# One mixture-of-experts stage: low halves on VectorE, all gates through DRAM, one ring of row tiles

## The chip, the cores and the metric

The kernel runs on one core of a Trainium2 chip. The metric is the device time of one execution in microseconds (us). A core has TensorE (PE, with its weight loads PEld), VectorE (DVE), ScalarE (ACT), GpSimd (POOL) and SyncE (SP); SP issues nearly all plain DMAs, POOL issues the indirect ones (gathers of table rows by index).

## The reference, cut to what matters

The model is two blocks of 512 tokens by 1024 features in float32. The change touches only the last layer of the second block, the retrieval of single-neuron experts, and what lies behind it:

```
q  = (t @ wq) ; sc = q . subkeys            # 512 tokens, 8 heads, 2 halves, 128 keys
s1,i1 = top_k(sc[half 0], 16) ; s2,i2 = top_k(sc[half 1], 16)
best,pos = top_k(s1 + s2, 16)               # of 256 sums
idx = e1 * 128 + e2 ; gate = softmax(best)  # 128 experts for each token, of 16384
act = gelu(u_tab[idx] . t) * gate
out = sum over the 128 of act * v_tab[idx]
```

## The kernel before

Every float32 product is made of three matmuls: an operand is split into a rounded high half (made by ACT, `hi`) and a low half, raw minus high (made by `lo`), and `mm3` adds high times high, high times low and low times high. `weight` (L266) loads one raw 128 x 1024 tile on SP's queue, makes the high half `wh` on ACT, and the low half `wl` on POOL, or on VectorE where the caller says so. L248 and L256 are the helper lines of the high and of the low half, whoever calls them.

The expert stage is `peer`. It treats the first 128 tokens and the other 384 (three groups `j` of 128) differently.

- Tokens 128 to 511 go the dense way: all 16384 experts in 128 blocks `b` of 128. `hidden(b)` multiplies the weight block `p_ut[b]` with the 384 tokens (24 matmuls of 384 columns into PSUM tile `H`) and ACT makes the gelu `Hg`. A dense gate matrix says how much each token wants of each expert. `gates` builds it, four tokens at a time (a gate group below): VectorE compares index rows with `iota` (tiles `o`, L1621, L1622, L1626), ACT scales two of the four (L1628), PE multiplies the one-hot tiles (`G`, L1629), ACT copies the result into `Gs` (L1630). There are 96 groups: three `j`, two halves of 64 tokens, 16 groups each; the halves use the two buffers `Gs0` and `Gs1`.
- Tokens 0 to 127 go the sparse way: `fetches` gathers, with indirect DMAs on POOL (L1566), 128 rows of `p_u` and 128 of `p_v`, each 128 x 1024; VectorE takes a dot product (L1571) or adds a scaled row to `y` (L1582).

Three parts follow each other. **Part A**, `topk`, to 2561 us: query products, maxima on VectorE. **Part B**, to about 2977 us: `decode` (indices and softmax), `gates`, and `hidden` of the first 72 blocks, each `Hg` written to DRAM (`dAct`). The gates of the first two `j` are written to DRAM (`dGate`), in eight writes of 512 KB for each half; those of the last `j` stay in `Gs0` and `Gs1`. **Part C**, to the end: for each block `b` one load of `p_v[b]`, the activation of the block (read back from `dAct` for b under 72, computed by `hidden` after that), times the gates, split (`ach`, `acl`), and 18 matmuls of 512 columns into six accumulators `acc`. The gate multiply is three VectorE instructions: 256 columns from `Gt` (L1479, read back for two blocks at a time) and twice 64 columns from `Gs0` and `Gs1` (L1482). In part C two of three `p_v` blocks have their low half on POOL, the third on VectorE; `p_ut` blocks always on POOL. About 1.15 rows are gathered per block at first, 3.03 per block from block 72, none after block 118.

The raw weights and the gathered rows share one ring of 7 tiles, `wr`; `wh` and `wl` have 4 tiles each. The program is written in the order of its stages; a scheduler then sets one fixed order for each engine and each queue, and every queue runs in order.

```
def lo(self, dst, src, hi, eng='dve'):
    e = self.nc.vector if eng == 'dve' else self.nc.gpsimd
    e.tensor_tensor(dst, src, hi.bitcast(F32), op=OP.subtract)
```

## Time and profile before

| | us |
|---|---|
| median of 3 runs (lowest, highest) | 3870.37 (3865.46, 3876.9) |
| the profiled execution: its time, its span | 3871.17, 3869.4 |
| busy in the span: PE, VectorE | 3500.6, 2833.6 |
| busy in the span: POOL, ACT | 1845.0, 1517.7 |
| mean granted TensorE clock | 0.953 of full |

What lies around the span is 1.8 us. The granted clock of a stretch is the mean over two levels: 1.0 is 2.4 GHz, 0.5 is 1.2 GHz. Busy times of PE are modelled and pipelined matmuls overlap, so its idle time is more telling than its busy time. A group's line names the line of the code, the engine, the operation, what it writes from what it reads with shapes, the count, the busy time in us, the mean of one in ns, and the idle time of the engine before it with what ended it. "DMA share" is the mean busy share of the core's 16 DMA engines.

### The profile page before, as it was taken

What the parts mean: (1) busy time and instruction counts of PE and PEld (TensorE: products, weight loads), DVE (VectorE), ACT (ScalarE), POOL (GpSimd) and SP (SyncE); (2) the same over time, 40 slices, a digit from 0 to 9 for tenths busy, and PEclk for the clock granted to TensorE, in tenths of its full rate; (3) what the DMA queues carried; (4) which work ended last, traced back from release to release, by engine and by line L of the source; (5) the groups of instructions that cost most, each with busy time, mean ns of one, the idle gap of its engine ahead of it and who ended that gap; (6) DMA issues with size and microseconds to landing.
All of it is one profiled execution on the core that took longest, in us unless ns stands there. A gap on an engine that the chain in (4) does not pass through costs nothing.

```text
span 3869.4 us, 51339 instructions
## 1 busy us (share of the span) xinstructions
PE 3500.6 (90%) x18415; PEld 2933.1 (76%) x18415; DVE 2833.6 (73%) x5128; ACT 1517.7 (39%) x2484; POOL 1845.0 (48%) x1039
## 2 busy tenths in 40 slices
PE   6889898999999669999999998997899999989988
PEld 4657667778888557788887976897798777777777
DVE  7895769777788893322496354889997899888884
ACT  4433573323323444323444443333676333222223
POOL 3763102222222444344346432566545676888773
PEclk9899898999999779999999998998999999999999
DMA  5442023344334444233323323245566898888782
GB/s 216 142 141 71 25 68 101 116 131 139 116 113 148 152 154 132 82 97 94 115 77 95 123 93 118 86 149 170 203 246 219 309 309 305 284 278 288 282 285 90
DMA packets 266992, 615.38 MB, mean 159 GB/s; under 512 B 39920, under 2 KB 132720, under 8 KB 263920
## 3 DMA queue, kind: packets, MB, share of 16 engines
q1 hardware_dynamic: 225232, 477.33, 37.1%
q0 software_dynamic: 36864, 134.23, 10.0%
q8 instruction: 145, 2.38, 0.3%
q10 hardware_dynamic: 4640, 0.53, 0.1%
q14 instruction: 111, 0.91, 0.1%
HBM read 539.26 MB, written 72.71 MB: 158 GB/s over the span
## 4 chain that ended last, share of the span: by engine, by line
PE 21%; DVE 9%; POOL 8%; issue 7%; DMA 4%; ACT 1%; POOLq 0%; ACTq 0%; DVEq 0%; SPq 0%
POOL wl L256 5%; PE mm L280 3%; PE mm L282 3%; PE mm L281 3%; POOL wr L1566 3%; DMA wr<-in_p_v_dram,idx 2%; PE H L282 2%; PE H L281 2%; PE H L280 2%; DVE o L1626 1%; PE acc L282 1%; PE acc L281 1%; PE acc L280 1%; PE G L1629 1%; DVE wr L1571 1%
## 5 line engine op out<-in xcount | busy, mean ns | idle before, releaser
L256 POOL TENSOR_TENSOR wl<-wr,wh 128x1024 fp32r<-128x1024 f32 x469 | 1172.4, 2503 | 1242.0 <-ACT wh L248 1137.0
L248 ACT ACTIVATE wh<-wr 128x1024 fp32r<-128x1024 f32 x512 | 536.8, 1053 | 724.5 <-PE mm L281 372.9
L280 PE MATMUL mm<-hh,wh 128*128 128x512 f32 (+1 forms) x1024 | 365.6, 362 | 25.1 <-DVE x L534 11.6
L282 PE MATMUL H<-wh,wl 128*128 128x384 f32 x1024 | 354.2, 346 | 17.8 <-POOL wl L256 16.8
L281 PE MATMUL mm<-hl,wh 128*128 128x512 f32 (+1 forms) x1024 | 366.3, 358 | 2.2 <-DVE hl L344 2.2
L282 PE MATMUL mm<-hh,wl 128*128 128x512 f32 (+1 forms) x1024 | 365.3, 358 | 1.6 <-POOL wl L256 1.6
L280 PE MATMUL H<-wh,wh 128*128 128x384 f32 x1024 | 349.9, 342 | 1.9 <-ACT Hg L1434 1.9
L281 PE MATMUL H<-wl,wh 128*128 128x384 f32 x1024 | 350.6, 342 | 0.0
L282 PE MATMUL acc<-wh,acl 128*128 128x512 f32 x768 | 310.1, 407 | 24.9 <-DVE acl L256 24.6
L280 PE MATMUL acc<-wh,ach 128*128 128x512 f32 x768 | 311.2, 405 | 20.7 <-ACT ach L248 20.7
L281 PE MATMUL acc<-wl,ach 128*128 128x512 f32 x768 | 308.3, 401 | 0.0
L1582 DVE SCALAR_TENSOR_TENSOR y<-wr,wgt,y 128x1024 f32<-128x1024 f32 x127 | 233.2, 1836 | 61.7 <-DMA wr<-in_p_v_dram,idx 61.3
L280 PE MATMUL mm<-fh,wh 128*128 128x512 f32 (+1 forms) x768 | 273.4, 357 | 5.0 <-DVE x L500 3.8
L281 PE MATMUL mm<-fl,wh 128*128 128x512 f32 (+1 forms) x768 | 273.5, 357 | 1.1 <-DVE fl L256 1.1
L282 PE MATMUL mm<-fh,wl 128*128 128x512 f32 (+1 forms) x768 | 272.3, 356 | 0.0
L280 PEld LDWEIGHTS mm<-hh,wh 128*128 128x128 f32 x1024 | 196.6, 193 | 64.6 <-DVE x L534 16.1
L1571 DVE SCALAR_TENSOR_TENSOR wr<-wr,tt 128x1024 f32<-128x1024 f32 x128 | 202.3, 1585 | 39.5 <-DMA wr<-in_p_u_dram,idx 25.2
L281 PEld LDWEIGHTS mm<-hl,wh 128*128 128x128 f32 x1024 | 197.3, 193 | 34.4 <-DVE hl L344 3.9
L282 PEld LDWEIGHTS mm<-hh,wl 128*128 128x128 f32 x1024 | 196.5, 192 | 30.7 <-POOL wl L256 2.4
L282 PEld LDWEIGHTS H<-wh,wl 128*128 128x128 f32 x1024 | 196.0, 191 | 27.6 <-POOL wl L256 27.4
L1566 POOL DMA_INDIRECT wr<-in_p_u_dram,idx x128 | 163.2, 1275 | 107.2 <-DVE wr L1571 42.1
L1566 POOL DMA_INDIRECT wr<-in_p_v_dram,idx x128 | 169.6, 1325 | 91.6 <-DVE y L1582 49.0
(684 smaller groups left out, 8519.4 us busy)
## 6 DMA issues: line engine op xcount, KB each, us to landing
wr<-in_mlp_w_dram SPq DMA_DIRECT2D x128, 512.0 KB, 3.6
wr<-in_p_ut_dram SPq DMA_DIRECT2D x128, 512.0 KB, 4.5
wr<-in_p_v_dram SPq DMA_DIRECT2D x128, 512.0 KB, 5.0
aw<-in_ada_w_dram SPq DMA_DIRECT2D x48, 512.0 KB, 3.6
wr<-in_ada_w_dram SPq DMA_DIRECT2D x32, 512.0 KB, 4.4
dGate<-Gs SPq DMA_DIRECT2D x32, 512.0 KB, 6.3
Gt<-dGate SPq DMA_DIRECT2D x64, 256.0 KB, 5.6
dAct<-Hg SPq DMA_DIRECT2D x72, 192.0 KB, 2.5
```

What stands on the lines that cost most here:

```text
L248: self.nc.scalar.activation(dst, src, AF.Copy, **({} if scale is None else {'scale': scale}))
L256: e.tensor_tensor(dst, src, hi.bitcast(F32), op=OP.subtract)
L280: mm(out, ah, bh, start=first, stop=False)
L281: mm(out, ah, bl, start=False, stop=False)
L282: mm(out, al, bh, start=False, stop=last)
L1566: gp.indirect_dma_start(out=r, out_offset=None, in_=tab, in_offset=bass.IndirectOffsetOnAxis(ap=idx[:, s:s + 1], axis=0))
L1571: v.scalar_tensor_tensor(r, r, 1.0, tt, op0=OP.mult, op1=OP.mult, accum_out=dots[:, s:s + 1])
L1582: v.scalar_tensor_tensor(y0, r, wgt[:, s:s + 1], y0, op0=OP.mult, op1=OP.add)
L1626: v.tensor_scalar(o1[:, t], iota, row, gate, op0=OP.is_equal, op1=OP.mult)
L1629: nc.tensor.matmul(p[:, t * 128:(t + 1) * 128], o2[:, t], o1[:, t], start=True, stop=True)
```

## The change

Five edits, in their effect on the program:

1. After `topk`, every low half of a weight is made on VectorE: 72 of `hidden` in part B, and in part C the 56 of `hidden` and the 85 of 128 `p_v` blocks that were on POOL. POOL keeps those of `topk` and the earlier layers.
2. The 16 multiplies of `decode` on 128 x 1024 tiles go from POOL to VectorE.
3. The gates of all three `j` go through DRAM: 16 more writes of 512 KB in part B.
4. In part C the gates of four blocks are read at once (768 KB per four blocks, before 256 KB per two), and the gate multiply of a block is one instruction of 384 columns, before three.
5. `Gs0` and `Gs1` end with part B. In their room part C has a ring of 13 tiles, `rw`, for raw `p_v` and `p_ut` blocks and gathered rows.

```diff
+        self.lo_eng = 'pool'
+        self.rows = None
...
-    def weight(self, ap, lo_eng='pool'):
-        raw = self.t(self.wp, [128, 1024], 'wr', F32, self.wb[0])
+    def row_tile(self):
+        pool, tag, bufs = self.rows or (self.wp, 'wr', self.wb[0])
+        return self.t(pool, [128, 1024], tag, F32, bufs)
+
+    def weight(self, ap, lo_eng=None):
+        lo_eng = lo_eng or self.lo_eng
+        raw = self.row_tile()
...
-            dG = tc.dram_tile([ND - 1, 2, 128, 128, 64], F32, name='dGate')
+            dG = tc.dram_tile([ND, 2, 128, 128, 64], F32, name='dGate')
...
-            G2 = [self.t(gp_, [128, 128, 64], f'Gs{i}') for i in range(2)]
             with ExitStack() as e1:
+                G2p = e1.enter_context(self.pool('pgs'))
+                G2 = [self.t(G2p, [128, 128, 64], f'Gs{i}') for i in range(2)]
...
                     cands = self.topk(tp, e2.enter_context(self.pool('pq', side='right')), hs)
+                self.lo_eng = 'dve'
...
-                        if j < ND - 1:
-                            for a in range(0, 128, 16):
-                                nc.sync.dma_start(dG[j, i, :, a:a + 16], G2[i][:, a:a + 16])
+                        for a in range(0, 128, 16):
+                            nc.sync.dma_start(dG[j, i, :, a:a + 16], G2[i][:, a:a + 16])
...
+                self.rows = e1.enter_context(self.pool('rows')), 'rw', 13
...
-                    if b % 2 == 0:
-                        G = self.t(tp, [128, 2 * (ND - 1), 2, 64], 'Gt', bufs=2)
-                        nc.sync.dma_start(G, dG[:, :, :, b:b + 2].rearrange('j i e a t -> e (j i) a t'))
+                    if b % 4 == 0:
+                        G = self.t(tp, [128, 2 * ND, 4, 64], 'Gt', bufs=2)
+                        nc.sync.dma_start(G, dG[:, :, :, b:b + 4].rearrange('j i e a t -> e (j i) a t'))
                         Gt.append(G)
-                    M = 128 * (ND - 1)
-                    Hm = H[:, :M].rearrange('e (j t) -> e j t', t=64)
-                    v.tensor_tensor(Hm, Hm, Gt[-1][:, :, b % 2], op=OP.mult)
-                    for i in range(2):
-                        ts = slice(M + 64 * i, M + 64 * i + 64)
-                        v.tensor_tensor(H[:, ts], H[:, ts], G2[i][:, b], op=OP.mult)
+                    Hm = H.rearrange('e (j t) -> e j t', t=64)
+                    v.tensor_tensor(Hm, Hm, Gt[-1][:, :, b % 4], op=OP.mult)
...
-                    wv = self.weight(I['p_v'][b * 128:(b + 1) * 128], 'pool' if b % 3 else 'dve')
+                    wv = self.weight(I['p_v'][b * 128:(b + 1) * 128])
...
-            r = self.t(self.wp, [128, D], 'wr', bufs=self.wb[0])
+            r = self.row_tile()
...
-                gp.tensor_tensor(oh.rearrange('p (h k) a -> p h k a', h=4), oh.rearrange('p (h k) a -> p h k a', h=4), atf[:, hs, i, None, :].to_broadcast([128, 4, K, K]), op=OP.mult)
+                v.tensor_tensor(oh.rearrange('p (h k) a -> p h k a', h=4), oh.rearrange('p (h k) a -> p h k a', h=4), atf[:, hs, i, None, :].to_broadcast([128, 4, K, K]), op=OP.mult)
```

The scheduler sets a new order from all this. In the rows below a name before `<-` is what is written, the names behind it what is read; numbers in names tell buffers apart.

TensorE at the end of part B, before (`H` is a block of `hidden`, `acc` the first block of part C):

```order
L281 MATMUL H_26456<-wl_20969,wh_26452 128x384
L282 MATMUL H_26456<-wh_20968,wl_26453 128x384
L280 MATMUL H_26456<-wh_20975,wh_26452 128x384
L281 MATMUL H_26456<-wl_20976,wh_26452 128x384
L282 MATMUL H_26456<-wh_20975,wl_26453 128x384
L280 MATMUL acc_26530<-wh_26553,ach_26547 128x512
L281 MATMUL acc_26530<-wl_26554,ach_26547 128x512
L282 MATMUL acc_26530<-wh_26553,acl_26548 128x512
L280 MATMUL acc_26531<-wh_26553,ach_26547 128x512
L280 MATMUL H_26490<-wh_20926,wh_26486 128x384
L281 MATMUL H_26490<-wl_20927,wh_26486 128x384
```

Before, all gate groups have gone by here, and the last block of `hidden` begins between the first matmuls of part C. The same place after, where the last block of `hidden` ends (`G` is one gate group):

```order
L289 MATMUL H_26509<-wh_20968,wl_26506 128x384
L287 MATMUL H_26509<-wh_20975,wh_26505 128x384
L288 MATMUL H_26509<-wl_20976,wh_26505 128x384
L289 MATMUL H_26509<-wh_20975,wl_26506 128x384
L1634 MATMUL G_23651<-o_4721_23652,o_4722_23653 128x128 x4
L1634 MATMUL G_23665<-o_4724_23666,o_4725_23667 128x128 x4
L1634 MATMUL G_23679<-o_4727_23680,o_4728_23681 128x128 x4
L1634 MATMUL G_23693<-o_4730_23694,o_4731_23695 128x128 x4
L1634 MATMUL G_23707<-o_4733_23708,o_4734_23709 128x128 x4
L1634 MATMUL G_23721<-o_4736_23722,o_4737_23723 128x128 x4
```

From there on the row holds 23 gate groups and no other matmul, to the first of part C:

```order
L1634 MATMUL G_23939<-o_4781_23940,o_4782_23941 128x128 x4
L1634 MATMUL G_23953<-o_4784_23954,o_4785_23955 128x128 x4
L1634 MATMUL G_23967<-o_4787_23968,o_4788_23969 128x128 x4
L287 MATMUL acc_26553<-wh_26574,ach_26568 128x512
L287 MATMUL acc_26554<-wh_26574,ach_26568 128x512
```

So `hidden` has moved ahead of the gates, and the last 23 groups stand alone.

SP's queue at the start of part C, before, with the semaphores that a DMA waits for (`DMAHW` with a digit is one of the eight that tell of landed SP transfers; `nf` is the weight of the final norm, `xf` the residual of the first 128 tokens):

```order
L270 DMA wr_26674<-in_p_v_dram 128x1024 [waits DMAHW6_49,Pool_49]
L1458 DMA dAct<-Hg_26334 128x384 [waits DMAHW7_49,Activation_49]
L270 DMA wr_26717<-in_p_v_dram 128x1024 [waits DMAHW0_49,Pool_49]
L1488 DMA nf_26536<-in_nf_w_dram 128x1024 [waits DMAHW1_49,PE_49]
L1490 DMA xf_26538<-dXs 128x8x128 [waits DVE_49,DMAHW2_49,PE_49,Activation_49]
L1530 DMA Hr_26540<-dAct 128x384 [waits DMAHW3_49,PE_49]
L1475 DMA Gt_26542<-dGate 128x4x128 [waits DMAHW4_49,PE_49]
L1530 DMA Hr_26557<-dAct 128x384 [waits DMAHW5_49]
```

The gate writes of the last `j` are not there, and five loads of `p_v` stand ahead of these rows. The same place after:

```order
L1463 DMA dGate<-Gs_4137_21001 128x1024 [waits DMAHW7_49]
L1463 DMA dGate<-Gs_4137_21001 128x1024 [waits DMAHW0_49]
L1493 DMA nf_26559<-in_nf_w_dram 128x1024 [waits DMAHW4_49,DMAHW5_49,DMAHW3_49,DMAHW6_49,DMAHW2_49,DMAHW7_49,DMAHW1_49,DMAHW0_49]
L1495 DMA xf_26561<-dXs 128x8x128 [waits PE_49]
L1535 DMA Hr_26563<-dAct 128x384
L1484 DMA Gt_26565<-dGate 128x6x256 [waits DVE_49,PE_49]
L277 DMA rw_26572<-in_p_v_dram 128x1024
L1535 DMA Hr_26578<-dAct 128x384
```

The last sixteen transfers ahead of `nf` are the gate writes of the last `j`, and `nf` now waits for all eight semaphores; the reads of `dAct`, of the gates and of `p_v` stand behind it.

VectorE in part C beyond block 72, before (L1571 is a dot product with a gathered row, L1479 and L1482 the gate multiply):

```order
L1571 SCALAR_TENSOR_TENSOR wr_30852,dots_20995<-wr_30852,tt_20892 128x1024
L1479 TENSOR_TENSOR Hg_30702<-Hg_30702,Gt_30635 128x256
L1482 TENSOR_TENSOR Hg_30702<-Hg_30702,Gs_4136_20997 128x64
L1482 TENSOR_TENSOR Hg_30702<-Hg_30702,Gs_4137_20998 128x64
L1571 SCALAR_TENSOR_TENSOR wr_30855,dots_20995<-wr_30855,tt_20892 128x1024
L256 TENSOR_TENSOR acl_30714<-Hg_30702,ach_30713 128x384
L1571 SCALAR_TENSOR_TENSOR wr_30883,dots_20995<-wr_30883,tt_20892 128x1024
L256 TENSOR_TENSOR wl_30889<-wr_30886,wh_30888 128x1024
L1571 SCALAR_TENSOR_TENSOR wr_30925,dots_20995<-wr_30925,tt_20892 128x1024
L1479 TENSOR_TENSOR Hg_30775<-Hg_30775,Gt_30783 128x256
```

The same stretch after, where L1576 and L1487 are those lines:

```order
L1487 TENSOR_TENSOR Hg_30497<-Hg_30497,Gt_30287 128x384
L1576 SCALAR_TENSOR_TENSOR rw_30814,dots_20995<-rw_30814,tt_20892 128x1024
L258 TENSOR_TENSOR acl_30507<-Hg_30497,ach_30506 128x384
L258 TENSOR_TENSOR wl_30613<-rw_30610,wh_30612 128x1024
L1576 SCALAR_TENSOR_TENSOR rw_30856,dots_20995<-rw_30856,tt_20892 128x1024
L1576 SCALAR_TENSOR_TENSOR rw_30859,dots_20995<-rw_30859,tt_20892 128x1024
L258 TENSOR_TENSOR wl_30678<-rw_30675,wh_30677 128x1024
L1487 TENSOR_TENSOR Hg_30568<-Hg_30568,Gt_30576 128x384
L1576 SCALAR_TENSOR_TENSOR rw_30887,dots_20995<-rw_30887,tt_20892 128x1024
L258 TENSOR_TENSOR acl_30580<-Hg_30568,ach_30579 128x384
L258 TENSOR_TENSOR wl_30684<-rw_30681,wh_30683 128x1024
```

The gate multiply is one row, and two low halves `wl` of 1024 columns stand in the queue for each block, between the rows that take gathered tiles.

## Rows read from the trace of the kernel before

**Rows 1.** The window view, six stretches: engines' busy time and instructions, granted clock, DMA share, GB/s

```profile
2561.00:2640.00 79.00, 61.24 (x334) 60.31 (x333) 67.89 (x88) 25.79 (x34) 56.66 (x28) 0.89 0.45 141
2640.00:2840.00 200.00, 166.84 (x992) 159.61 (x991) 195.72 (x287) 117.49 (x205) 117.38 (x55) 0.91 0.55 186
2840.00:2966.00 126.00, 117.34 (x793) 113.99 (x793) 112.67 (x206) 96.69 (x178) 62.08 (x30) 1.00 0.63 220
2966.00:3320.00 354.00, 335.60 (x1439) 267.71 (x1438) 314.26 (x435) 112.18 (x155) 238.17 (x133) 0.98 0.90 309
3320.00:3761.00 441.00, 400.38 (x1888) 340.45 (x1888) 378.82 (x393) 129.04 (x184) 362.53 (x211) 0.98 0.82 284
3761.00:3869.00 108.00, 94.79 (x471) 84.13 (x470) 47.45 (x77) 38.77 (x60) 41.56 (x17) 0.97 0.32 109
```

**Rows 2.** Groups by line, whole span: instruction, count, busy us, mean ns, idle before, releaser

```profile
L256 POOL TENSOR_TENSOR wl<-wr,wh 128x1024 fp32r<-128x1024 f32 x469 | 1172.4, 2503 | 1242.0 <-ACT wh L248 1137.0 <-DMA dP<-s_pt 31.1 <-PE mm L281 23.8
...
L1630 ACT ACTIVATE Gs<-G 128x512 f32<-128x512 f32 x96 | 100.0, 1089 | 3.5 <-PE G L1629 3.5
...
L1628 ACT ACTIVATE o<-o,ct 128x128 f32<-128x128 f32 x192 | 65.9, 393 | 84.4 <-DVE o L1622 84.3
```

**Rows 3.** VectorE instructions: duration ns min/median/max, first and last start us; gate tiles

```profile
L1626 DVE TENSOR_SCALAR o<-c_iota,ct x192: 329/335/5356, 2663.7 to 2959.6; 128x128 f32<-128x128 f32 x192
...
L1622 DVE TENSOR_TENSOR o<-c_iota,ct x96: 406/411/2612, 2663.4 to 2959.0; 128x256 f32<-128x256 f32 x96
```

**Rows 4.** The same view of the splitting line L256

```profile
L256 DVE TENSOR_TENSOR acl<-Hr,ach x72: 543/547/3068, 2977.3 to 3314.5; 128x384 fp32r<-128x384 f32 x72
...
L256 DVE TENSOR_TENSOR acl<-Hg,ach x56: 542/549/2753, 3326.7 to 3851.7; 128x384 fp32r<-128x384 f32 x56
L256 DVE TENSOR_TENSOR wl<-wr,wh x43: 1210/1214/3377, 2974.9 to 3834.0; 128x1024 fp32r<-128x1024 f32 x43
```

**Rows 5.** The timeline from 2904 to 2909 us: start, duration, engine, instruction

```profile
2904.18 0.68 DVE L1621 TENSOR_TENSOR o<-c_iota,ct 128x512 f32<-128x512 f32 x1
...
2904.31 1.05 PE L1629 MATMUL G<-o,o 128*128 128x128 f32 x8
...
2907.79 3.14 POOL L256 TENSOR_TENSOR wl<-wr,wh 128x1024 fp32r<-128x1024 f32 x1 [3.84 <-ACT wh L248]
...
2908.60 2.87 DVE L1621 TENSOR_TENSOR o<-c_iota,ct 128x512 f32<-128x512 f32 x1
```

**Rows 6.** Groups by line of VectorE, 2561 to 2966 us

```profile
L1626 DVE TENSOR_SCALAR o<-c_iota,ct 128x128 f32<-128x128 f32 x192 | 118.9, 658 | 0.0
L1621 DVE TENSOR_TENSOR o<-c_iota,ct 128x512 f32<-128x512 f32 x96 | 78.3, 816 | 1.7 <-ACT ct L1608 1.5 <-PE G L1629 0.2
L1571 DVE SCALAR_TENSOR_TENSOR wr<-wr,tt 128x1024 f32<-128x1024 f32 x32 | 49.2, 1536 | 9.2 <-issue 9.2
...
L1720 DVE TENSOR_TENSOR k_oh<-k_f,c_iota 128x1024 f32<-128x1024 f32 x16 | 28.0, 1751 | 0.1
...
L1704 DVE TENSOR_SCALAR k_pi<-k_pos 128x128 uint32<-128x128 uint32 x16 | 17.1, 1075 | 0.1
```

**Rows 7.** Groups by line of VectorE, 2966 to 3761 us

```profile
L1582 DVE SCALAR_TENSOR_TENSOR y<-wr,wgt,y 128x1024 f32<-128x1024 f32 x122 | 225.9, 1852 | 56.7 <-DMA wr<-in_p_v_dram,idx 56.3
L1571 DVE SCALAR_TENSOR_TENSOR wr<-wr,tt 128x1024 f32<-128x1024 f32 x96 | 153.1, 1602 | 30.2 <-DMA wr<-in_p_u_dram,idx 25.2 <-issue 4.9
```

**Rows 8.** Who waited for whom, 3320 to 3761 us: total us, times, longest

```profile
PEld H L282 <- POOL wl L256: 24.0, 28, 2.2
```

**Rows 9.** The tiles H (to 2980 us) and y: as in rows 3

```profile
L282 PE MATMUL H<-wh,wl x570: 331/334/667, 2507.1 to 2980.0; 128*128 128x384 f32 x190
...
L1582 DVE SCALAR_TENSOR_TENSOR y<-wr,wgt,y x127: 1268/1279/5901, 2935.4 to 3761.2; 128x1024 f32<-128x1024 f32 x127
```

**Rows 10.** Landing of the gate writes (tile Gs); then a 5 us window, columns as in rows 1

```profile
DMA to landing us min/median/max: 2.6/6.3/12.1
...
2980.00:2985.00 5.00, 5.00 (x28) 4.68 (x28) 3.93 (x3) 2.15 (x4) 3.09 (x3) 1.00 1.06 389
```

## The prediction

> **What bounds the kernel now.** I read the window view first, to find what each stretch waits for, then the groups and the timeline behind it. The change begins behind the top-k, so all before 2561 us stays. TensorE is the engine with the most work to the end: it is idle 17.8, 33.2 and 8.7 us in the three windows of part B (79, 200 and 126 us less its busy time), 18.4 in the next and 40.6 in the one after [rows 1]. So 60 us of part B and 59 of part C to 3761 us can be won at most, and in part B some 22 us more, since the granted clock is 0.89 and 0.91 in its first two windows (11% of 61 and 9% of 167 us). The last 108 us have few gathers and are left as they are.
>
> Why does TensorE wait? VectorE is near full where TensorE is not: 195.7 of 200 us from 2640 on, 379 of 441 from 3320 on [rows 1]. But much of that is stall. The first compare of a gate group takes 0.68 us; the same instruction takes 2.87 where it starts 0.81 us behind a POOL low half of 3.14 us, and both end together [rows 5]. The short compares have a median of 0.335 us and a maximum of 5.356 [rows 3]. A POOL low half takes 2.5 us in the mean [rows 2], on VectorE 1.214 in the median [rows 4].
>
> The Trainium skill, "SBUF — State Buffer", section "Who interferes with whom", says that a VectorE instruction with two SBUF inputs, or in a two-port mode, and a GpSimd instruction that reads SBUF exclude each other for the whole of an instruction. The timeline's pair agrees. By that rule the stalls go with POOL's arithmetic; were they VectorE's own, the 106 us that are worked out below would stay, and the sum would be near 3900.
>
> **Part B, step by step.** Removed: stalls. Count times (mean less undisturbed duration) gives for the five largest groups 192 x 0.323 = 62 us, 96 x 0.136 = 13, 32 x 0.326 = 10 (1.21 being the duration of any 1024-column instruction), 16 x 0.54 = 9 and 16 x 0.74 = 12 (against the 0.335 of another 128-column one) [rows 3, 4, 6]: 106 us. Added on VectorE: 72 low halves and 16 multiplies of decode at 1.214 [rows 4], 87 + 19 = 106 us. VectorE's load is the same, 376 us in 405 [rows 1]; but 18 of the low halves now stand among the top-k's instructions (22 us), so 354 are left, and the gates could end at 2561 + 354 = 2915. TensorE no longer waits for POOL.
>
> TensorE: the last `hidden` matmul now starts at 2980.0 [rows 9]. In the new order 23 gate groups stand behind it that stood ahead; a group holds TensorE 1.05 us [rows 5], so 24 us leave the stretch. If none of the idle and clock loss of 82 us returns, `hidden` ends at 2956; if all, at 2874. I take half, 41 us, since VectorE stays over 90% loaded in fixed order: 2915.
>
> Then comes a stretch that did not exist: 23 groups alone. ACT sets their pace, two scalings of 0.393 and a copy of 1.089 [rows 2], 1.875 us each: 43 us, to 2958. VectorE needs less (0.68 + 0.41 + 2 x 0.335 = 1.76 [rows 3, 5]). The last eight gate writes land up to 12.1 us after their issue [rows 10]: 2970. SP's queue is held at `nf` until all have landed, and behind it stand `nf`, `xf`, `Hr`, `Gt` and the first raw block, 512 + 512 + 192 + 768 + 512 KB = 2.56 MB. At 309 GB/s, the mean of the next part [rows 1], that is 8.3 us, at the 389 of a short window [rows 10] 6.6. With the split behind it the first activations are ready near 2980, where this now happens at 2977.3 (first `acl`) [rows 4]. So the gain of part B is spent on its tail; the bounds are 2939 and 3021. POOL's gathers wait at the same place for the same landings; they have the whole of part C.
>
> **Part C to block 72** now takes 349 us (`acl` from 2977.3 to 3326.7 [rows 4]). On TensorE 18 us of idle time and some 4 us of the last `hidden` block go: 327 at the least. DMA is the other limit: its share is 0.90 [rows 1], 314 us of all 16 engines. The gates of the last `j` add 64 KB per block, 4.7 MB in 72 blocks, 15 us at 309 GB/s: 328. At a share of 0.90 that would be 364 us, at the 1.06 of a short window [rows 10] 309. The ring of 13 keeps more loads waiting, so I take 0.95: 345 us.
>
> **Part C from block 72 to the last gather** takes 434 us (3326.7 to 3761.2 [rows 4, 9]). TensorE's idle 41 us leave 393. Its largest single wait of this stretch by POOL, 24.0 us of weight loads behind `wl` [rows 8], goes with POOL's part. VectorE per block: multiply and split 0.55 each, 3.03 gathered rows at 1.21 to 1.28, two low halves at 1.214 [rows 4, 9]: 7.3 us, against 9.4 now per block (434/46). DMA: 0.82 x 434 = 356, and 3 MB more, 8 at that share: 364 us, or 404 at a share of 0.90. I take 403: three quarters of the idle time go, the rest stays with DMA. What hides the 1.21 us low halves is VectorE's free 2 us a block; without it they would cost 46 x 2.4 = 112 us.
>
> **The sum**, against the profiled execution (span 3869.4, time 3871.2, median of three 3870.4): 2980 + 345 + 403 + 108 = 3836, and 1.8 around the span: **3838 us**, 33 less. Its own range goes half way to the bounds of each term, 20 + 9 + 5 us down and 21 + 10 + 1 up, less a little since they seldom fall together: 3808 to 3866.
>
> **The rivals.**
>
> *Part C runs at TensorE's floor.* The ring lifts the DMA share to that of the short window, and nothing of the idle time stays: 2980 + 327 + 393 + 108 + 2 = 3810. For it: 389 GB/s were moved at 2980 us, where five loads of `p_v` had been queued [rows 10]. Against it: the share of 0.90 holds over 354 us.
>
> *Part B gives nothing back.* VectorE stays the fuller engine there, every low half of `hidden` now waits its turn behind compares, and the tail is paid in full: `hidden` ends at 2956, part C begins at 3021, and 3021 + 345 + 403 + 108 + 2 = 3879, no change. For it: a load of 376 us that does not fall. Against it: 18 halves that are done early, and 195.7 busy us of 200 from 2640 on [rows 1] show that VectorE can run full.
>
> *VectorE's single file makes TensorE wait for gathers: slower.* In part C VectorE stands idle 56.3 and 25.2 us for gathered rows [rows 7]. Until now POOL's low halves went on meanwhile; now they queue behind the waiting instruction. If all 82 us reach TensorE, part C to the last gather is 327 + 393 + 82 = 802 and the end 2980 + 802 + 108 + 2 = 3892. It is slower from 72 of these 82 us on (3882 is 0.3% above). Against it: with 13 tiles, at five rows per block, a gather can be issued 2.6 blocks or some 23 us ahead, with 7 tiles 1.4 blocks.
>
> **How the numbers follow.** Forecast 0.50, TensorE's floor 0.20, part B without gain 0.15, single file 0.15. A measurement of this kernel tells about 0.3% from no change, 3859 to 3882. The forecast and the floor lie below that: faster 0.70; same 0.15; slower 0.15. The range of 8 in 10 leaves out the lower half of the floor case and the upper part of the single file: 3800 to 3888.
>
> **What the profile after will show.** Right: no POOL arithmetic behind 2561 us, and the short compare's maximum under 1 us; `hidden` ending near 2915, then some 43 us with TensorE mostly idle, a granted clock below 1.0, and a stop until near 2980; TensorE's idle time from 3327 on a quarter of 41 us; a DMA share near 0.95 before block 72. Wrong: compares that still stretch beside gathers (then the stalls were not POOL's arithmetic); a first `acl` beyond 3000 (the tail was mis-sized); VectorE's waits for gathered rows above 82 us, with TensorE's waits for `wl` behind them. The costliest guesses are the half of 82 us and the share of 0.95, 41 and some 18 us.

## The result, and the profile after

| | before | after |
|---|---|---|
| median (lowest, highest), us | 3872.9 (3865.5, 3876.9) | 3777.1 (3774.4, 3779.6) |
| first `acl` of part C | 2977.3 | 2943.4 |
| first `acl` of block 72 | 3326.7 | 3294.1 |
| last `acl` | 3851.7 | 3754.8 |

The ratio is 0.9755, with a 95% interval of 0.9736 to 0.9773: 96 us less, where 33 were forecast. The profiled execution took 3774.4 us with a span of 3772.6. The kernel is faster, and the gain was put nearly three times too small.

The window view of after, cut where its parts end, answers to [rows 1]. Columns: stretch and its length, then busy us and instructions of PE, PEld, DVE, ACT and POOL, granted clock, DMA share, GB/s. The fifth row ends where block 116 begins (3663.1 us), as the fifth of before nearly does (at 3761, where block 116 begins at 3762.4).

```profile
2561.00:2640.00 79.00, 78.57 (x454) 78.28 (x453) 72.89 (x175) 33.03 (x44) 17.33 (x15) 1.00 0.60 202
2640.00:2840.00 200.00, 199.84 (x1314) 199.48 (x1313) 191.89 (x379) 147.72 (x254) 35.26 (x24) 1.00 0.75 258
2840.00:2943.00 103.00, 64.57 (x452) 60.57 (x450) 59.22 (x155) 66.36 (x127) 6.58 (x7) 0.85 0.53 202
2943.00:3294.00 351.00, 323.79 (x1367) 258.56 (x1368) 273.60 (x367) 115.77 (x153) 116.08 (x93) 0.97 0.96 346
...
3294.00:3663.00 369.00, 369.00 (x1847) 332.82 (x1847) 297.25 (x355) 132.78 (x179) 152.14 (x123) 1.00 0.93 332
```

TensorE is now busy all but 0.6 us from 2561 to 2840 us (before, 228 of 279), and without a gap from block 72 to the last `acl`. What it waits for ahead of that lies between 2840 and 3294 us.

The view by line of after, with durations in ns (min/median/max), first and last start, answers to [rows 3, 4, 9]:

```profile
L1631 DVE TENSOR_SCALAR o<-c_iota,ct x192: 332/341/354, 2652.8 to 2907.8; 128x128 f32<-128x128 f32 x192
...
L258 DVE TENSOR_TENSOR acl<-Hr,ach x72: 545/551/561, 2943.4 to 3284.2; 128x384 fp32r<-128x384 f32 x72
L258 DVE TENSOR_TENSOR acl<-Hg,ach x56: 547/550/559, 3294.1 to 3754.8; 128x384 fp32r<-128x384 f32 x56
...
L1587 DVE SCALAR_TENSOR_TENSOR y<-rw,wgt,y x127: 1271/1277/1285, 2946.4 to 3647.3; 128x1024 f32<-128x1024 f32 x127
```

The long ends are gone in all of these rows: the short compare's longest was 5356 ns and is 354, that of `y` was 5901 and is 1285. In part C POOL has nothing left but gathers.

### The profile page after: what moved, and what is told of

It reads as the page before. It is cut to its first block, busy times and chain, and to the rows that moved or that the text cites. A ratio compares the mean times of both kernels' runs of the same rounds, so it can differ in the third digit from the quotient of the medians.

```text
span 3772.6 us, 50694 instructions
## 1 busy us (share of the span) xinstructions
PE 3457.0 (92%) x18415; PEld 2923.8 (78%) x18415; DVE 2665.1 (71%) x5101; ACT 1531.7 (41%) x2484; POOL 1263.9 (34%) x810
## 5 line engine op out<-in xcount | busy, mean ns | idle before, releaser
L258 POOL TENSOR_TENSOR wl<-wr,wh 128x1024 fp32r<-128x1024 f32 (+1 forms) x256 | 636.4, 2489 | 1061.4 <-ACT wh L250 995.3
L250 ACT ACTIVATE wh<-wr 128x1024 fp32r<-128x1024 f32 x328 | 346.3, 1056 | 643.1 <-PE mm L288 358.5
L250 ACT ACTIVATE wh<-rw 128x1024 fp32r<-128x1024 f32 x184 | 195.1, 1060 | 374.9 <-PE acc L289 197.1
L289 PE MATMUL H<-wh,wl 128*128 128x384 f32 x1024 | 345.6, 337 | 0.0
L258 DVE TENSOR_TENSOR wl<-rw,wh 128x1024 fp32r<-128x1024 f32 x184 | 225.2, 1224 | 169.2 <-ACT wh L250 168.9
L1571 POOL DMA_INDIRECT rw<-in_p_v_dram,idx x127 | 156.4, 1231 | 350.2 <-DMA dGate<-Gs 107.4
L289 PE MATMUL acc<-wh,acl 128*128 128x512 f32 x768 | 252.1, 398 | 0.6 <-DVE acl L258 0.6
L287 PEld LDWEIGHTS acc<-wh,ach 128*128 128x128 f32 x768 | 146.9, 192 | 96.2 <-ACT wh L250 34.6
L287 PEld LDWEIGHTS H<-wh,wh 128*128 128x128 f32 x1024 | 192.5, 188 | 2.8
```

Source lines behind the costliest of these rows:

```text
L250: self.nc.scalar.activation(dst, src, AF.Copy, **({} if scale is None else {'scale': scale}))
L287: mm(out, ah, bh, start=first, stop=False)
L289: mm(out, al, bh, start=False, stop=last)
L1571: gp.indirect_dma_start(out=r, out_offset=None, in_=tab, in_offset=bass.IndirectOffsetOnAxis(ap=idx[:, s:s + 1], axis=0))
```

## The experiments

Medians with the ratio to before; "first `acl`", "block 72" and "last `acl`" are the starts of the first `acl<-Hr`, the first `acl<-Hg` and the last one. These three are of the profiled execution alone; in e4_lowonly that took 3821.9 us, 11 less than the median, and in e11_rate16 3835.0, 6 more.

| kernel | median us | ratio (95%) | first `acl` | block 72 | last `acl` |
|---|---|---|---|---|---|
| after | 3777.1 | 0.9755 (0.9736 to 0.9773) | 2943.4 | 3294.1 | 3754.8 |
| e1_poolC | 3823.8 | 0.9861 (0.9841 to 0.9881) | 2949.6 | 3309.1 | 3806.6 |
| e3_poolB | 3832.6 | 0.9887 (0.9865 to 0.9909) | 2996.9 | 3357.7 | 3814.7 |
| e6_dummy | 3997.9 | 1.0325 (1.0308 to 1.0342) | 2941.0 | 3467.4 | 3977.3 |
| e4_lowonly | 3832.6 | 0.9888 (0.9868 to 0.9908) | 2925.5 | 3276.7 | 3802.3 |
| e5_gates | 3863.3 | 0.9979 (0.9966 to 0.9991) | 3005.0 | 3336.1 | 3849.6 |
| e14_form | 3741.0 | 0.9658 (0.9642 to 0.9674) | 2930.1 | 3261.3 | 3721.9 |
| e11_rate16 | 3828.8 | 0.9861 (0.9834 to 0.9887) | 2944.2 | 3273.7 | 3815.6 |
| e2_noring | 3758.7 | 0.9695 (0.9675 to 0.9715) | 2948.2 | 3277.2 | 3737.4 |
| e9_ring7 | 3734.5 | 0.9643 (0.9627 to 0.9659) | 2939.1 | 3256.0 | 3715.4 |
| e7_rate09 | 3759.5 | 0.9700 (0.9678 to 0.9721) | 2943.8 | 3277.6 | 3738.4 |
| e13_hr6 | 3755.8 | 0.9686 (0.9665 to 0.9706) | 2944.2 | 3273.8 | 3734.7 |

Two theories stood at the start. *Stalls*: POOL's arithmetic stretched VectorE's instructions, and that it is gone is the gain. *Ring*: the ring of 13 lets gathers run ahead, and that is the gain behind block 72.

### POOL's arithmetic: put back in part C, put back in part B, and added for nothing

**e1_poolC**, part C's low halves on POOL again:

```diff
                 self.rows = e1.enter_context(self.pool('rows')), 'rw', 13
+                self.lo_eng = 'pool'
...
-                    wv = self.weight(I['p_v'][b * 128:(b + 1) * 128])
+                    wv = self.weight(I['p_v'][b * 128:(b + 1) * 128], 'pool' if b % 3 else 'dve')
```

> The kernel after, but in part C POOL again makes the low halves that it made before (all of p_ut, two of three of p_v); ring of 13 and the dense gates stay. Theory 'VectorE's stalls' (POOL's arithmetic beside VectorE's was the cost, and its end is what part C gained): from block 72 on a block takes about 9.4 us again instead of the 8.42 of after, so 46 x 1.0 = 46 us, and a few us before block 72, which is bound by transfers: 3820 to 3835 us, with `acl` and y of VectorE stretched beyond 2 us again. Theory 'the ring' (gathers that run ahead of VectorE were the gain of part C): within 5 us of after, 3772 to 3782.

Measured: 47 us more than after, 52 by the profiled executions' last `acl`. From block 72 to the last `acl` it took 497.5 us (after 460.7, before 525.0), so 37 of the 52 are lost there; 6 are lost ahead of part C and 9 before block 72. The view by line and a group of POOL, of e1_poolC:

```profile
L1588 DVE SCALAR_TENSOR_TENSOR y<-rw,wgt,y x127: 1272/1285/4096, 2952.5 to 3706.8; 128x1024 f32<-128x1024 f32 x127
...
L258 POOL TENSOR_TENSOR wl<-rw,wh 128x1024 fp32r<-128x1024 f32 x123 | 317.8, 2585 | 37.5 <-ACT wh L250 35.7
```

The stretched `y` is back with the low halves, and the time lies in the range of "stalls". "Ring" expected 5 us at most and falls for this part: the ring of 13 is in this kernel. But what TensorE waits for from 3300 to 3640 us says more (its weight loads; total us, times, longest):

```profile
PEld H L289 <- POOL wl L258: 24.5, 19, 2.6
PEld acc L289 <- DVE acl L258: 1.9, 1, 1.9
```

Behind block 72 nearly all of these waits end with a low half of POOL, and not with a stretched instruction of VectorE. So a second reading stands beside "stalls": POOL's low half, 2585 ns in the mean, comes late by itself. e6_dummy, below, asks about it.

**e3_poolB**, low halves and decode's multiplies of part B on POOL again:

```diff
                     cands = self.topk(tp, e2.enter_context(self.pool('pq', side='right')), hs)
-                self.lo_eng = 'dve'
...
                 self.rows = e1.enter_context(self.pool('rows')), 'rw', 13
+                self.lo_eng = 'dve'
...
-                v.tensor_tensor(oh.rearrange('p (h k) a -> p h k a', h=4), oh.rearrange('p (h k) a -> p h k a', h=4), atf[:, hs, i, None, :].to_broadcast([128, 4, K, K]), op=OP.mult)
+                gp.tensor_tensor(oh.rearrange('p (h k) a -> p h k a', h=4), oh.rearrange('p (h k) a -> p h k a', h=4), atf[:, hs, i, None, :].to_broadcast([128, 4, K, K]), op=OP.mult)
```

> The kernel after, but in part B the low halves of p_ut and the multiplies of decode are on POOL again, in the old order among the gates; part C as after. Theory 'VectorE's stalls': the short compares stretch again, `hidden` ends near 2950 in place of 2876 and the first `acl` comes at 2970 to 2985 in place of 2943: 27 to 42 us more, 3804 to 3819. Theory 'the work only moved' (VectorE has the same 376 us with either, so nothing of part B's gain is the stalls'; it came from the order of gates and `hidden`): within 5 us of after if the order is the cause and is kept, and the compares stay at 0.33 us.

Measured: 55.5 us more than after, above the range expected. The view by line of e3_poolB (`H` up to 2998 us):

```profile
L1631 DVE TENSOR_SCALAR o<-c_iota,ct x192: 333/340/5353, 2666.5 to 2959.9; 128x128 f32<-128x128 f32 x192
...
L289 PE MATMUL H<-wh,wl x410: 331/334/667, 2600.2 to 2979.4; 128*128 128x384 f32 x137
...
L258 DVE TENSOR_TENSOR acl<-Hr,ach x72: 550/554/560, 2996.9 to 3340.3; 128x384 fp32r<-128x384 f32 x72
```

The last matmul of `hidden` starts at 2979.4, 4 us before that of the kernel before (2983.1; the 2980.0 of [rows 9] is the edge of that view's window). The first `acl` comes at 2996.9, 53.5 us behind that of after and 19.6 behind that of before. So all that part B gains goes when POOL's arithmetic comes back, and the dense gates cost some 20 us at the hand-over, from the end of the last gate copy to the first `acl`: 33 us here, 12 before.

TensorE's largest wait in part B of the kernel before, 2600 to 2966 us, was for the short compare:

```profile
PE G L1629 <- DVE o L1626: 37.2, 23, 6.1
```

e3_poolB has this wait again (33.1 us, 17 times, up to 6.1), after has none. The fixed order comes back too: here and before, `hidden` ends behind the last gate group, in after 32 us ahead of it. No run has the one without the other, so how much of part B's gain is the order's stays open.

**e6_dummy**, the kernel after with POOL work added that nobody reads:

```diff
+                junk = self.t(tp, [128, D], 'junk')
+                def idle():
+                    gp.tensor_tensor(junk, tt, nf, op=OP.subtract)
...
                         H = hidden(b)
+                        idle()
...
+                    if b % 3:
+                        idle()
```

> The kernel after with useless work added: wherever the kernel before had a POOL low half in part C, POOL makes one subtraction over 128 x 1024, whose result nobody reads. The low halves stay on VectorE. It tells two readings of the 47 us apart that POOL's low halves in part C cost beside the kernel after. 'Stalls': VectorE's instructions stretch beside POOL's as they did with the low halves, acl and y beyond 2 us, and part C loses 25 to 55 us: 3802 to 3832. 'Late low half' (POOL took 2.5 us in place of 1.2 for a half that TensorE waited for): nobody waits for these, so 5 us at most: 3775 to 3782.

Measured: 221 us more than after, far above either number. Groups of e6_dummy, 2941 us onward (busy us, mean ns, idle before):

```profile
L258 DVE TENSOR_TENSOR wl<-rw,wh 128x1024 fp32r<-128x1024 f32 x120 | 250.2, 2086 | 11.8 <-ACT wh L250 11.7
L1594 DVE SCALAR_TENSOR_TENSOR y<-rw,wgt,y 128x1024 f32<-128x1024 f32 x81 | 159.6, 1971 | 1.2 <-DMA rw<-in_p_v_dram,idx 0.8
L258 DVE TENSOR_TENSOR acl<-Hr,ach 128x384 fp32r<-128x384 f32 x72 | 90.8, 1272 | 8.3 <-ACT ach L250 8.3
...
L1499 POOL TENSOR_TENSOR junk<-tt,nf 128x1024 f32<-128x1024 f32 x139 | 352.8, 2538 | 4.0
```

These are VectorE's instructions of after (1225, 1277 and 551 ns) at 1.5 to 2.3 times the length, and the idle time before them is small: VectorE is full (506 of 526 us before block 72), at some half of its speed. So stalls are enough to cost this much, and "late low half" falls as the whole account, since POOL makes no low half here. In e1_poolC both are at work, and nearly all of TensorE's waits behind block 72 end with the late halves; how its 47 us divide stays open.

The 141 instructions cost 221 / 141 = 1.57 us each, of the 2.54 that one takes. That is more than POOL's low halves cost in e1_poolC. There VectorE was rid of 141 x 1.21 = 171 us of work at the same time, and 221 - 171 = 50 is near the 47; that this is the reason was not tried. The places differ too: 104 of the 139 in the view run before block 72, where 176 of the 221 us are lost, while of e1_poolC's 123 low halves some 50 run there.

### What the low halves and the gates give alone

**e4_lowonly**, the kernel before with edits 1 and 2 alone (the multiply of `decode` as in the change, not shown again):

```diff
                     cands = self.topk(tp, e2.enter_context(self.pool('pq', side='right')), hs)
+                self.lo_eng = 'dve'
...
-                    wv = self.weight(I['p_v'][b * 128:(b + 1) * 128], 'pool' if b % 3 else 'dve')
+                    wv = self.weight(I['p_v'][b * 128:(b + 1) * 128])
```

> The kernel before with nothing changed but the engine of the low halves and of the multiplies of decode behind the top-k: VectorE in place of POOL. Gates of the last j stay in SBUF with their own multiplies in part C, gathered rows keep their 7 tiles. Theory 'VectorE's stalls': this alone gives most of the 96 us, 60 to 85: 3788 to 3813. Theory 'the ring and the merged gates matter': half or less, 3825 to 3850, and part C from block 72 stays above 9 us per block, VectorE waiting for gathered rows. Single file: no gain or slower, above 3860.

Measured: 0.9888, 43 us less than before, as the second theory expected; that the ring is not what is missing, e2_noring below shows. The first `acl` comes 52 us earlier, which is all of the gain; block 72 to the last `acl` takes 525.6 us, as before (525.0), although no instruction is stretched there (`y` takes 1358 ns at the most). What ended VectorE's and POOL's waits from 3277 to 3706 us in e4_lowonly (total us, times, longest):

```profile
DVE y L1585 <- DMA wr<-in_p_v_dram,idx: 73.3, 49, 3.7
DVE wr L1574 <- DMA wr<-in_p_u_dram,idx: 39.8, 32, 3.9
...
POOL wr L1569 <- DVE y L1585: 113.9, 29, 6.8
POOL wr L1569 <- DVE wr L1574: 69.1, 22, 7.5
```

VectorE waits 113 us for gathered rows, and POOL waits for VectorE to free a tile for the next gather; TensorE's weight loads wait 27.1 us for `acl` and 21.4 for `wl` of VectorE in this stretch. That is what the rival "single file" of the prediction describes.

**e5_gates**, edits 3 and 4 alone (the kernel after without edits 1, 2 and 5):

> The kernel before with the gates' part of the change alone: all gates go through DRAM, one multiply per block; the low halves and the multiplies of decode stay on POOL, rows and raw weights share 7 tiles. 'Stalls' (VectorE's stalls behind POOL are what part B lost, and half of what part C lost): part B stays as slow as in the kernel before, and its tail grows by the writes of the last j: first `acl` at 2985 to 3005; part C from block 72 at 9.0 to 9.5 us per block: 3860 to 3890, no gain. 'Merged gates' (the multiply and the larger reads are what part C gained, whatever POOL does): below 8.7 us per block from 72 on and 3815 to 3835.

Measured: 0.9979, 9 us less than before, at the edge of what can be told. The first `acl` comes at 3005.0, 28 us later than before; 18 of these come back before block 72 (331.1 us for 349.4) and 11 behind it (513.5 to the last `acl`). So the gates alone give next to nothing, the low halves alone 43 us, and both without the ring (e2_noring, below) 118: what they give together is not the sum.

**e14_form** asks whether it is the form of the gates' product: it is e9_ring7 (below, 3734.5 us) with three multiplies and reads for two blocks, as before.

```diff
-                    if b % 4 == 0:
-                        G = self.t(tp, [128, 2 * ND, 4, 64], 'Gt', bufs=2)
...
+                    if b % 2 == 0:
+                        G = self.t(tp, [128, 2 * ND, 2, 64], 'Gt', bufs=2)
...
-                    v.tensor_tensor(Hm, Hm, Gt[-1][:, :, b % 4], op=OP.mult)
+                    for js in (slice(0, 2 * ND - 2), slice(2 * ND - 2, 2 * ND - 1), slice(2 * ND - 1, 2 * ND)):
+                        v.tensor_tensor(Hm[:, js], Hm[:, js], Gt[-1][:, js, b % 2], op=OP.mult)
```

> The kernel after with the ring cut to 7 (3734.5 us), and with the gates' product in part C in the old form: three multiplies per block (256, 64 and 64 columns) and reads of the gates two blocks at a time. It asks why the low halves on VectorE alone (e4_lowonly) left a block behind block 72 at 9.5 us and this kernel has 8.4. 'Form' (three multiplies and smaller reads cost the block): 9 us or more per block there, 3760 and above. 'Order' (there raw weights sit in the ring some two blocks ahead and leave few tiles to the gathers; here they don't, in either form): 8.4 to 8.5 us per block, and 3733 to 3742.

Measured: 3741.0, and from block 72 TensorE is as full as in after. The window of e14_form:

```profile
3261.00:3629.00 368.00, 368.00 (x1843) 332.03 (x1842) 311.44 (x456) 130.28 (x180) 167.65 (x132) 1.00 0.94 336
```

So the form alone is not it, with the ring in its new place; that the old place alone is not it either, e2_noring below shows. What also differs is how long raw weights sit in the ring. Pairing loads with low halves and gathers with their use, for those issued between 3340 and 3560 us, a raw tile is held from its load's issue to the end of its low half for 21.5 us in e4_lowonly, 12.7 in e14_form and 11.4 in e9_ring7; a gathered row from issue to use 6.6, 9.4 and 10.0 us. At 9.56 us per block, raw weights then hold 2 x 21.5 / 9.56 = 4.5 of e4_lowonly's 7 tiles, and 3.03 x 6.6 / 9.56 = 2.1 are left to gathers, which took some 6 us each to land in the kernel before.

**e11_rate16** was to test this: e4_lowonly with fewer rows left for the time behind block 72.

```diff
-                more = (256 - 1.15 * NA - 0.7 * (NA - 24)) / (2 * (118 - NA))
+                more = (256 - 1.6 * NA - 0.7 * (NA - 24)) / (2 * (118 - NA))
...
-                    fetches(1.15 if b < NA else more)
+                    fetches(1.6 if b < NA else more)
```

> The kernel before with VectorE's low halves alone (e4_lowonly), but 1.6 rows gathered per block before block 72 in place of 1.15, so that behind it about 2.2 per block remain in place of 3. In e4_lowonly a block takes 9.5 us there although VectorE has a quarter of its time free. 'Held tiles': raw weights stay 21 us each in the ring of 7 (two per block: 43 tile-us), a gathered row 6.6; with 2.2 rows 58 tile-us are left of 63, so a block takes 8.4 to 8.9 us: 30 to 55 us less behind block 72, and before it 20 to 45 more for the 16 MB that come earlier. 'Gates' (the three multiplies hold a block up): 9.3 to 9.6 us per block as before.

Measured: 3828.8, not to be told from e4_lowonly's 3832.6. Block 72 begins at 3273.7 (3276.7 in e4_lowonly), so the rows that come earlier cost nothing up to there, though the first `acl` is 19 us later; behind it 541.9 us, 9.85 per block, so both numbers are missed. That it is slower there than with more rows can't be told, since the two profiled executions lie 6 us above and 11 below their medians. Raw weights were held still longer, 28.3 us, and took the tiles that the gathers no longer claimed. So the time that a tile is held is no fixed cost, and with it the arithmetic of my expectation falls. That raw weights far ahead starve the gathers in e4_lowonly fits these four kernels, but it is argued, not shown; why the fixed order lets them stand so far ahead there was not tried. So it stays open what the gates' edits add behind block 72.

### The ring

**e2_noring**, the kernel after on the old ring of 7:

```diff
-                self.rows = e1.enter_context(self.pool('rows')), 'rw', 13
```

> The kernel after without its ring of 13: gathered rows and raw weights share a pool of 7 tiles, as gathered rows had before. Theory 'VectorE's stalls': what the ring gives is small, 0 to 8 us: 3777 to 3785, VectorE's waits for gathered rows under 30 us. Theory 'the ring': the 32 us by which part C from block 72 to the end came out below my forecast are the ring's, so 3800 to 3815, with a last y at about 3690 in place of 3647. My recorded rival (VectorE in single file waits for gathers) would show here: up to 80 us of waits of y for rw, and an end beyond 3840.

Measured: 18 us *less* than after, where both theories expected more time. From block 72 it is the same (460.2 us); before it, 329.0 us for 350.7; the first `acl` comes 5 us later. The recorded rival does not show, with 7 tiles and the gates' edits: no time is lost behind block 72.

**e9_ring7**, the ring in its new place, with 7 tiles:

```diff
-                self.rows = e1.enter_context(self.pool('rows')), 'rw', 13
+                self.rows = e1.enter_context(self.pool('rows')), 'rw', 7
```

> The kernel after with its ring cut from 13 tiles to 7, in the same place. Without the ring (rows and raw weights in the old 7 tiles) the kernel ran 18 us faster. 'Place': the new ring lies where the gates' staging tiles lay, so POOL's first gather into it waits 107 us for the last gate write to land, and 8 of its gathers then crowd the first loads of part C; with 7 tiles in that place it stays so: 3765 to 3778, and POOL again waits over 90 us for dGate. 'Depth': 13 tiles let gathers run 10 rows ahead (5 MB, 15 us at 340 GB/s) while transfers are the limit before block 72; with 7 in any place this goes: 3755 to 3763.

Measured: 42.6 us less than after, better than either theory allowed. First `acl` 4 us earlier, 316.9 us to block 72 (34 less), 459.4 from there. The window from 2943 to 3000 us, part C's first 57 us in after, which begins 4 us into part C in e9_ring7; by the view of DMA issues, the loads issued around the hand-over (KB, median us to landing); and the longest waits of POOL and of TensorE, first of after (issues 2918 to 2945 us):

```profile
2943.00:3000.00 57.00, 44.71 (x190) 35.57 (x190) 46.48 (x54) 17.52 (x22) 22.01 (x16) 0.89 1.04 396
...
rw<-in_p_v_dram SPq DMA_DIRECT2D x5, 512.0 KB, 15.0
...
Hr<-dAct SPq DMA_DIRECT2D x3, 192.0 KB, 16.3
...
rw<-in_p_v_dram,idx POOLq DMA_INDIRECT x7, 9.6
...
POOL rw L1571 <- DMA dGate<-Gs: 107.4, 1, 107.4
...
PE acc L287 <- ACT wh L250: 34.4, 1, 34.4
```

then of e9_ring7 (issues 2910 to 2945 us):

```profile
2943.00:3000.00 57.00, 57.00 (x266) 46.88 (x265) 46.31 (x56) 20.05 (x26) 22.28 (x16) 0.98 1.03 384
...
rw<-in_p_v_dram SPq DMA_DIRECT2D x5, 512.0 KB, 7.9
...
Hr<-dAct SPq DMA_DIRECT2D x5, 192.0 KB, 7.0
...
rw<-in_p_v_dram,idx POOLq DMA_INDIRECT x3, 6.0
...
POOL rw L1571 <- ACT o L1633: 84.4, 1, 84.4
...
PE acc L287 <- ACT wh L250: 24.7, 1, 24.7
```

Two things cost the ring of 13 its time. At the hand-over: the 13 tiles reach over `Gs`, so POOL's first gather into them waits 107.4 us for the last gate write, and then seven gathers go out, from 2924 to 2932 us, beside the first loads of part C, which begin with `nf` at 2923.3 and land after 15 and 16 us. With 7 tiles POOL waits for something that ends earlier: four gathers go out from 2906 to 2912, ahead of `nf` at 2928.4, the next one at 2943.4 (the three in the row are the last two of these and that one), and the loads land after 7 to 8. TensorE's wait between its last gate group and part C is 10 us shorter. After that: SP's queue. Its order in after, then in e9_ring7 (the fourth `Hr` is the activation of block 3):

```
DMA Hr_26612<-dAct 128x384
DMA xr_26637<-dXs 128x384
DMA rw_26645<-in_p_v_dram 128x1024
DMA xr_26676<-dXs 128x384
DMA rw_26687<-in_p_v_dram 128x1024
DMA Gt_26695<-dGate 128x6x256
DMA rw_26728<-in_p_v_dram 128x1024
DMA rw_26767<-in_p_v_dram 128x1024
DMA Hr_26651<-dAct 128x384
```

```
DMA Hr_26612<-dAct 128x384
DMA xr_26637<-dXs 128x384
DMA rw_26645<-in_p_v_dram 128x1024
DMA xr_26676<-dXs 128x384
DMA Gt_26695<-dGate 128x6x256
DMA Hr_26651<-dAct 128x384
DMA rw_26687<-in_p_v_dram 128x1024
```

Activations have three buffers, so they can't be queued further ahead than three blocks; raw weights with a long ring can, and stand in front of them. The next two kernels ask whether this or the bytes alone delay the blocks.

e9_ring7 is also 24 us faster than e2_noring, with as many tiles in another place: 9 at the first `acl`, 12 before block 72. There the gathers are not held back, and the last gate copy ends 8 us later (2925.0 for 2916.7); what the place costs beyond that was not tried.

**e7_rate09**, fewer rows before block 72:

```diff
-                more = (256 - 1.15 * NA - 0.7 * (NA - 24)) / (2 * (118 - NA))
+                more = (256 - 0.9 * NA - 0.7 * (NA - 24)) / (2 * (118 - NA))
...
-                    fetches(1.15 if b < NA else more)
+                    fetches(0.9 if b < NA else more)
```

> The kernel after, with its ring of 13, but before block 72 it gathers 0.9 rows per block in place of 1.15 (the rest later). The ring cut to 7 made the kernel 42 us faster, 34 of it before block 72. 'Bytes': the longer ring lets more rows be gathered while transfers are the limit; 0.25 x 72 = 18 rows or 9.4 MB less there are 25 us at 370 GB/s: 3748 to 3756, and TensorE's waits for activations (29 us) gone. 'Queue order': the ring lets raw weights be queued on SP six blocks ahead, while activations have three buffers, so each `Hr` stands behind several 512 KB loads; fewer gathers change little of that: 3764 to 3777.

**e13_hr6**, activations as far ahead as raw weights:

```diff
-                        H = self.t(tp, [128, N], 'Hr', bufs=3)
+                        H = self.t(tp, [128, N], 'Hr', bufs=6)
```

> The kernel after, with its ring of 13, but with six buffers for the activations read back (`Hr`) in place of three, so that SP issues each before the raw weights of the same block. 'Queue order': part C before block 72 falls from 351 to 317 to 330 us, as with the ring of 7, and the whole to 3738 to 3756. 'Bytes': the same bytes at the same places, so 3770 to 3780.

Measured: 17.5 and 21.3 us less than after; both lie between, or at the edge of, what the two theories said. TensorE's waits from 3000 to 3300 us, in after and then in e7_rate09:

```profile
PE acc L287 <- ACT ach L250: 19.5, 9, 4.6
```

```profile
PE acc L287 <- ACT ach L250: 3.5, 1, 3.5
```

In e13_hr6 and e9_ring7 that view has no such row. So one wait, 20 us for activations that come late, is removed by either cure: fewer bytes, or the same bytes in a better order. That nearly the same bytes run without it (97 gathers from 2920 us to block 72, 100 in after) shows that the order is enough. Why fewer bytes (84 gathers) are enough too is not shown: the DMA share from 3000 us to block 72 is 0.94 in e7_rate09 and 0.95 in after. The other half, at the hand-over, neither of them touches: TensorE's wait for part C is 32.5 and 34.1 us, and from 2943 to 3000 us it is busy for 45.7, in after for 44.7, in e9_ring7 for 57. That the seven gathers are the cause there is read from the rows above; no run took them away alone.

### More blocks ahead

TensorE is idle for some 40 us between the end of `hidden` and part C. Three kernels put more blocks there, by `self.spilled`: 80 without the ring (e8_na80), 76 with the ring of 7 (e12_na76), and that with the loads `nf` and `xf` moved behind block 16 (e15_best).

> The kernel after without the ring, and with 80 in place of 72 blocks computed ahead of part C. The stretch from 2872 us to the first accumulation near 2948 leaves TensorE idle for some 40 us; 8 blocks of 4.2 us fit there. Expected: 34 us less from block 72 to the end of part C, of which the tail gives 10 to 17 us back (ACT has 8 more activations and high halves in it): 3735 to 3748. If the tail is bound by ACT and DMA more than I think, 3750 to 3762 and nothing is won.

> The kernel after with the ring cut to 7 (3734.5 us) and 76 in place of 72 blocks computed ahead. 80 in place of 72, without the ring, gave 6 us for the 34 that I had expected, since the gates' end, and with it the first accumulation, moved by 23 us. With 4 blocks more: the tail moves by some 10 us, part C falls by 17: 3725 to 3732; if the tail moves by as much as part C falls, 3733 to 3740.

> The kernel after with the ring cut to 7 and 76 blocks ahead (3730.6 us), and with the two loads of 512 KB that stand on SP ahead of part C's first activation (`nf`, `xf`) moved behind block 16, where their data are still 100 blocks early. If they are part of the hand-over, 2.7 to 3.4 us at 309 to 389 GB/s come off: 3727 to 3729. If the hand-over waits for the gate writes and the raw weights alone, nothing changes: 3729 to 3735.

Measured: 3752.6 (0.9687, 0.9665 to 0.9709), 3730.6 (0.9618, 0.9598 to 0.9637) and 3733.2 us (0.9631, 0.9615 to 0.9647). Eight blocks more gave 6 us for 34: the first `acl` moved from 2948.2 to 2970.8. Four more moved it by 18 us and gave 4. Both gains lie within the intervals. Moving 1 MB out of the hand-over gave nothing that can be told. The ring of 7, with 72 or 76 blocks, is the fastest version: 43 to 47 us faster than after.

## Why the prediction was wrong, step by step

**The cause was right, as far as it goes.** The forecast said that VectorE's stalls are POOL's arithmetic and go with it; e1_poolC, e3_poolB and e6_dummy show it from three sides. Even the size was met: the five groups of its 106 us took 291.5 us before ([rows 6]) and 184.9 in after, 106.6 less. One reading of [rows 5] was not: the compare and the low half do not end together; the compare ends at 2911.47, 0.54 us behind the low half, so most of its 0.68 us ran behind it. Behind block 72 the end of the stalls was not enough: e4_lowonly has none and gains nothing there, and e1_poolC gives back 37 of the 64 us won there, with TensorE's waits for POOL's low halves at 24.5 us as they were at 24.0 before ([rows 8]). The Trainium skill, "SBUF — State Buffer", section "Who interferes with whom", was weighed against the reading that the stalls are VectorE's own (a sum near 3900): the trace agrees with the page, 354 ns for 5356 at the longest compare, and the sum by the other reading is out. What failed are the terms of the sum that turn the freed time into a gain: 2980 + 345 + 403 + 108 stands against 2943 + 351 + 369 + 110.

**Part B: the half of 82 us.** `hidden` was to end at 2915, with 2874 if all of the idle time and clock loss came back. All came back: from the 2983.1 at which it really ended before, the same sum gives 2877. The last matmul of `hidden` in part B, and the last copy of a gate group, in after:

```profile
L289 PE MATMUL H<-wh,wl x405: 332/334/423, 2599.9 to 2877.8; 128*128 128x384 f32 x135
...
L1635 ACT ACTIVATE Gs<-G x96: 1025/1096/1163, 2656.8 to 2910.5; 128x512 f32<-128x512 f32 x96
```

The step that failed is the half itself, taken since VectorE stays over 90% loaded. It does, at 192 of 200 us from 2640 on, and TensorE has not one us of idle time beside it. The load was not what TensorE waited for: 37.2 us of its waits ended with short compares, single ones of which were stretched to 5.4 us, and these are gone. 37 us of the miss.

**The tail and the hand-over.** The gate groups alone took 34 us, not 43, to the end of the last copy at 2911.5; ACT was their pace, busy for 33.4 of 33.6 us, but its instructions overlap: 23 copies of 1.063 and 42 scalings of 0.385 us add up to 40.6. The hand-over took 32, not 22. The loads behind the gate writes were priced at 6.6 to 8.3 us for 2.56 MB alone, and of POOL's gathers, held at the same place, the text said that they have the whole of part C. They were released at that moment and went out beside those loads (seven rows, 3.5 MB, landing at 15 us for the raw weights). These two errors cancel by luck.

**Part C to block 72: 345 forecast, 351 measured.** The share of 0.95 was met (0.96), the 345 nearly, by luck: the reason was turned round. The deeper ring was to lift the share and gain by it; with 7 tiles the share is higher still, and the 13 cost 34 us. e9_ring7 needs 316.9 us, less than my floor of 327:

```profile
2943.00:3256.00 313.00, 313.00 (x1365) 253.56 (x1364) 256.44 (x343) 110.43 (x148) 100.54 (x86) 1.00 0.99 363
```

More loads in flight are no gain when the wrong ones are in front.

**Block 72 to the last gather: 403 forecast, 369 measured**, to block 116 (the last `y` itself comes at 3647.3 now). Two errors. A quarter of the idle time was left to DMA; none stayed, at a share of 0.93. And the floor of 393 was too high by 24, since it took TensorE's busy time of a stalled stretch for the work. [Rows 1] had the means: 400.38 us for 1888 instructions there are 212 ns each, 94.79 for 471 in the last stretch 201; after has 369.00 / 1847 = 200. By the last stretch's rate the floor is 1888 x 201 ns = 380 for the 441 us, 374 for the 434. The Trainium skill, "Perfetto Trace Analysis", section "Identifying the Most-Contended Engine", warns that matmul busy time is a poor measure of how near a kernel is to its limit, and names the weight loads' busy time as one to use; the trace agrees, with 340.45 / 1888 = 180 ns per load before and 332.82 / 1847 = 180 after.

**The last 108 us** were 110, as forecast.

**The rivals.** TensorE's floor came true from block 72 on, with a lower floor than its price, but not by the ring that was to bring it: e2_noring has the same 460 us without it. "Part B gives nothing back" is out. "Single file" did not happen in after (VectorE waits under 1 us for gathered rows in part C), but in e4_lowonly the waits are as it said, and nothing is gained behind block 72. The number of tiles, which the prediction held against it, does not decide: e2_noring and e9_ring7 have 7 as e4_lowonly does, and lose nothing there. What does decide stays open.

## What to carry to other kernels

A full engine need not hold up another: VectorE was busy for 98% of the 200 us from 2640 on before and for 96% after, and TensorE's waits went with the single long instructions. So ask which instruction ends a wait, not how loaded its engine is. Take an engine's floor from a stretch in which it never waits, not from its busy time in one in which it does. And a longer ring is not free: here it let the largest loads be queued ahead of small ones that have few buffers, and where it lay decided when its first users started; 7 tiles beat 13 by 43 us.

## What the runs showed that was not expected

One useless POOL subtraction over 128 x 1024, which nobody waits for, cost the kernel 1.57 us in the mean, and 141 of them 221 us; that kernel takes 3% longer than the one before, in which POOL made useful low halves. POOL's gathers do nothing of the kind: 123 of them, 152 us of POOL's time between 3294 and 3663 us, leave `y` at 1285 ns at the most.
